# A one-core decoder step: scores with zero-padded queries, heads convolved in pairs, stores behind loads, filler matmuls, shared sample tiles

## The chip, the cores and the metric

The kernel runs on one core of one Trainium2 chip. The metric is the device time of one execution in microseconds (us); the executions shown agree within 0.3%. PE is TensorE, DVE VectorE, ACT ScalarE, POOL GpSimd; SP is the engine from whose queue all DMAs are issued here.

## The reference

One inference step of a hybrid decoder layer: a prompt of 512 tokens and eight samples of four tokens, 544 rows of width 1024 in all.

```python
shift, scale, gate = split(silu(c) @ w_cond + b_cond, 3)
h = x * (1 + scale) + shift
qa, ka, va, za, qkv_b, zb, a_b, b_b, g_a, g_b = h @ w_in          # 11280 columns
# branch A: dilated sliding-window softmax attention, 3 groups of 8 heads of 64,
#   (window, dilation) = (128, 1), (512, 4), (2048, 16); the groups merged by softmax share; * silu(za)
# branch B: causal convolution of width 4 + silu on q, k, v; gated delta rule over 8 heads of 128,
#   exact, in chunks; RMS norm per head; * silu(zb)
merged = sigmoid(g_a) * (yA @ w_branch_a) + sigmoid(g_b) * (yB @ w_branch_b)
y = layer_norm(ALPHA * x + gate * (merged @ w_out))
```

It also returns the key and value rows of the windows (those of the samples are the caches moved on by four rows, the bulk of the writes), the last three rows ahead of the convolution, and the delta states.

## The kernel before

The kernel doesn't issue instructions as its Python runs. `Recorder` (line 246) records every operation with its tiles; `schedule` (line 426) then plans all five engines with a cost model of its own, and `emit` (line 644) issues each engine's operations in the planned order. That is why every instruction of the profile has line 663. At each step the planner takes the engine that is free first, and on it the ready operation with the lowest rank, then the earliest recorded. Ranks: 0 the recurrence of branch B, 1 its blocks, 2 gates and preparation, 3 prompt attention, 4 early sample attention, 9 the stream of projections (on engines other than PE these go first, rank -1), 30 the copies of the caches. On PE an operation of another array mode than the present one may be held back for up to `HOLD`, 1 us of the plan. The threads of the recording (`Threads`, line 673) are interleaved by a clock that counts planned PE time.

**The stream.** `jobs` (line 1978) holds one entry for each 128 columns of the projection. A job loads 512 KB of weights (`wt`, three buffers), splits them into a rounded part and a rest (`hi` on ACT, `lo` on DVE, two buffers each), and multiplies them with `hhi` and `hlo`, the split activations, in two halves of 272 columns, 24 matmuls each. Each half goes to one of the two banks of `pp` and is copied out by `evac`. The order of jobs before: head 0 of branch B, then for each of four head pairs j nine attention jobs (query, key, value of three groups), with heads 1, 2 after the first nine, 3, 4 after the second, 5, 6 after the third, and head 7 between the sixth and the seventh of the last nine. The jobs for `za`, `zb` and the gates follow.

**The front.** Eight modulation tiles `wm` of 1 MB are loaded and multiplied (`cond_product`), the activations made from the result, and the first three jobs run ahead, tile by tile.

**Branch B.** `conv_job` (line 1085) copies a projection into `ext` (two buffers), convolves it on DVE into `acc` (two buffers), and writes head h's `KQ` (two buffers) or `uv` (one buffer). `delta_blocks` (line 1133) prepares the 128-row chunks; `delta_rule` (line 1244) runs the recurrence over four chunks, head after head. The job that makes the first part of head h starts, in the recording, when head h-2 is through.

**Branch A.** `attention_job` (line 1380) copies query, key and value out: for groups 1 and 2 in a permuted order. The 128 rows of a tile are two heads of 64. `scores` (line 1433) takes for each head the rows `hp` of query and key, a contraction of 64 rows, so PE is in a mode of half its rows (64\*128 in the profile; other matmuls of 128 rows are 128\*128). Sixteen steps of six such matmuls, each in two passes, make 192 records. After probabilities, transposes and value products the groups are merged with weights that go through DRAM (`dw`, `wv`).

**Samples.** `sample_attention` (line 1601) runs twice; the early one keeps its tiles in nine slabs of `opool` and, for `Qz` and `PTa`, in a pool `s0`.

Of the kernel before, what the change touches and what calls it, by code (L numbers as in the profile page):

```python
# [21 lines left out]
SEQ = 512  # L22
# [223 lines left out]
class Recorder:  # L246
# [5 lines left out]
    AGAIN = {"pe": 0.0, "ve": 0.11, "se": 0.14, "ge": 0.11, "sp": 0.0}  # L252
    HOLD = 1.0
    ENTER = {(128, 128): 0.197, (64, 128): 0.197, (64, 64): 0.142, (32, 32): 0.073, (128, 64): 0.1, (128, 32): 0.0,
             (64, 32): 0.1, (32, 128): 0.2, (32, 64): 0.1}
# [3 lines left out]
    def __init__(self):  # L259
        self.ops, self.events, self.rank, self.now, self.idle = [], [], 0, 0.0, 0.0  # L260
        self.group = None
        self.hold = self.HOLD
        self.scratch = {}


# [79 lines left out]
    def cost(self, op, args):  # L345
# [35 lines left out]
        elif e == "se":  # L381
            c = (0.155 if in_psum else 0.21) + 0.83e-3 * n
            a = (0.07 if "accum_out" in op.kw else 0.0) + (0.08 if pointer else 0.0)
            op.cost, op.late = c - 0.1 + a, 0.1
            f = args[2]
# [5 lines left out]
        else:  # L391
# [20 lines left out]
            if not dram[0]:  # L412
                per, op.extra = run / 23.3e3, 1.75
# [9 lines left out]
            op.cost, op.late, op.table = 0.53 if dram[0] and dram[1] else 0.42, 0.0, None  # L423


    def schedule(self):
# [30 lines left out]
        avail = {e: [] for e in self.ENGINES}  # L457
        free = {e: 0.0 for e in self.ENGINES}
        port, queue, table = {"ve": 0.0, "ge": 0.0}, {True: 0.0, False: 0.0}, None
# [64 lines left out]
        while done < len(ops):  # L524
            best = None
            for e in self.ENGINES:
# [111 lines left out]
        events()  # L638
        self.span = max(op.done for op in ops)

    def margin(self, p, op):
# [74 lines left out]
def body(ctx, tc, io):  # L716
# [47 lines left out]
    ones = consts.tile([128, 128], F32, name="ones")  # L764
    ve.memset(ones, 1.0)
    small = consts.tile([128, 4], F32, name="small")
    bnw, hbnw, eps4, eps1 = (small[:, i:i + 1] for i in range(4))
# [44 lines left out]
    with ExitStack() as fctx:  # L812
# [14 lines left out]
        for k in range(KT):  # L827
            sp.dma_start(wm[k], io["w_mod"][k])
            if k == 0:
                sp.dma_start(cst, io["const"])  # L830
            if k % 2 == 0:
                sp.dma_start(xT[:, k:k + 2], io["xT"][:, k:k + 2])
            if k in FIRST:
                i = FIRST.index(k)
                raws[i] = wraw.tile([128, D], F32, name="wt", tag="wraw")
                sp.dma_start(raws[i], io["w_in"][TILE_AT["b", 0, (1, 0, 2)[i]]])
        sp.dma_start(wab, io["w_ab"])
        sp.dma_start(tables["g"], io["const_g"])
# [294 lines left out]
    def delta_blocks(h):  # L1133
# [14 lines left out]
        rcf = rc.rearrange("p a c -> p (a c)")  # L1148
        kr = dl.tile([128, 4, 128], F32, name="kr")
        for s in range(2):  # L1150
# [3 lines left out]
            sq = dl.tile([128, 4, 128], F32, name="sq", bufs=1)  # L1154
            for c in range(4):
                se.activation(sq[:, c], cols128(pt)[:, c], AF.Square, accum_out=rc[:, s, c:c + 1])
            if s == 0:
                ve.tensor_copy(kr, cols128(pt))
            yield 2.2 + 2 * s
# [13 lines left out]
        yield 1.0  # L1173
        QKd = dl.tile([128, 4, 128], F32, name="QKd")
        ve.tensor_mul(QKd, NTs, cols128(rb[:, 1]))
# [204 lines left out]
    def attention_job(j, g, s):  # L1380

        def begin():
            pairs[j][s, g] = spare()[:, :SEQ] if s == 2 else ap.tile([128, 512], F32, name="qk"[s], bufs=3)

        def evac(n, ps):
            t, scale = pairs[j][s, g], 1.0 if s else -0.125
            if g == 0:
                lo, hi = ((0, 272), (272, 512))[n]
                se.activation(t[:, lo:hi], ps[:, 0:hi - lo], AF.Copy, scale=scale)
            else:  # L1390
                v = t.rearrange("p (r a n) -> p n a r", r=4, a=4)
                m = (17, 15)[n]
                se.activation(v[:, 17 * n:17 * n + m], ps[:, 0:16 * m].rearrange("p (n a r) -> p n a r", a=4, r=4),
                              AF.Copy, scale=scale)
            if n:
# [6 lines left out]
    def prompt_attention():  # L1402

        for j in range(4):
            qt, kt, vrow = {}, {}, {}
            for g in range(3):
                yield ready[j, g]
                qt[g], kt[g], vt = (pairs[j][s, g] for s in range(3))
                vrow[g] = ap.tile([128, 4, 128], F32, name="vrow", bufs=3)
# [23 lines left out]
            def scores(i):  # L1433
# [4 lines left out]
                for g in range(3):  # L1438
                    for hh in range(2):
                        hp = slice(64 * hh, 64 * hh + 64)  # L1440
                        if g == 0:
                            pe.matmul(pS[hh][:, k0:256], qt[0][hp, tk], kt[0][hp, 128 * (i - 1) + k0:128 * (i + 1)],
                                              start=True, stop=True)
# [157 lines left out]
    def sample_attention(T, t, stream, W, pace_of, by, over):  # L1601


        cols = slice(256 * T, 256 * T + 256)
        Qz = t["Qz"].rearrange("p (g j i h) -> p g j i h", g=3, j=2, h=4)
        ge.memset(Qz, 0.0)
        for jl in range(2):
            for hh in range(2):
                hp = slice(64 * hh, 64 * hh + 64)
                ge.tensor_copy(Qz[hp, :, jl, :, 2 * jl + hh], qs[hp, 2 * T + jl])  # L1610

# [42 lines left out]
        for jl in range(2):  # L1654
            for x in range(1024 // W):
                kt = kts[jl, x]
                for bl in range(0, nb, 2):
                    b = nb * x + bl
                    pe.matmul(pS[16 * b:16 * b + 32, 0:256], Qz[:, 0, jl, 4 * b:4 * b + 8].rearrange("p i h -> p (i h)"),
                              kt[:, 128 * bl:128 * bl + 256], start=(jl == 0), stop=(jl == 1), tile_position=(0, 16 * b))  # L1660
        for g in range(3):
            for jl in range(2):
                for bp in range(4):
                    pe.matmul(pS[32 * bp:32 * bp + 32, 256 + 32 * g:288 + 32 * g],
                              Qz[:, g, jl, 8 * bp:8 * bp + 8].rearrange("p i h -> p (i h)"), ks[:, 2 * T + jl, g, :],
                              start=(jl == 0), stop=(jl == 1), tile_position=(0, 32 * bp))
# [68 lines left out]
    def early_tiles():  # L1735

        slab = [op.tile([128, NT], F32, name="slab", tag="o") for _ in range(9)]
        t = {}
        for i, names in ((4, ("Sa", "qr", "sst")), (5, ("Sb", "od", "o2")), (6, ("sba", "PTn")), (7, ("sbb", "om")), (8, ("knv",))):
# [237 lines left out]

    for s in (1, 0, 2):
        jobs.append(conv_job(0, s))
    h = 1  # L1980
    for j in range(4):
        nine = [attention_job(j, g, s) for g in range(3) for s in range(3)]
        if j == 3:
            jobs += nine[:6] + [conv_job(7, s) for s in (1, 0, 2)] + nine[6:]
        else:
# [17 lines left out]
    ap = pool(actx, "ap", 1)  # L2003
    s0ctx = ExitStack()
    s0 = pool(s0ctx, "s0", 1)
    threads.set(began, 0.0)
# [18 lines left out]
    threads.run(lambda: not threads.parts)  # L2025
    s0ctx.close()
    actx.close()
# [12 lines left out]
    def samples():  # L2040
        yield from sample_decays(op.tile([128, NT], F32, name="nd", tag="o"))
        yield from sample_delta()
        s1 = pool(sctx1, "s1", 1)
        yield from sample_attention(1, {n: qr1 if n == "qr" else s1.tile([128, w], F32, name=n) for n, w in SHAPES.items()},
                                    lambda: s2.tile([128, D], F32, name="kv", tag="cache"), 1024, 2.0, (ve,), late_over)
# [248 lines left out]
```

## Time and profile before

| | us |
|---|---|
| median of three runs | 958.55 (956.23 to 959.11) |
| the profiled execution | 957.46 |
| its span, first to last instruction | 955.5 |
| PE busy | 915.9 |
| DVE busy | 738.5 |
| ACT busy | 417.6 |
| POOL busy | 61.9 |

Granted clock of PE over the span: 0.984. Bytes read from HBM 220.49 MB, written 103.70 MB. In a row of the profile stand the engine, the operation, the tiles written and read, the shapes and a count; fp32 matmuls take two passes and so appear twice. Durations of matmuls overlap, since they are pipelined: what one costs is seen from start to start.

### The profile page before, as it was taken

Reading aid. Unit: us, or ns where it says so; the run is one execution under the profiler, and the core shown is the slowest. Engines: PE = TensorE matmul, PEld = TensorE weight load, DVE = VectorE, ACT = ScalarE, POOL = GpSimd, SP = SyncE. Lnnn points to the kernel's source line nnn. Section 1 sums busy time; section 2 is a strip of 40 time slices with the busy share of each in tenths; the row PEclk is TensorE's granted clock in tenths of the full one; section 3 lists DMA queues with packets and bytes.
Section 4 is the critical chain, followed back from the end, with each engine's and each line's share of the span. In section 5 each row is a group of like instructions: output and inputs, shape, how many; then the busy total and the mean of one; then the engine's idle time right before and its main releaser. Section 6 shows DMA issues by size and latency. Waiting matters only on the chain.

```text
span 955.5 us, 20831 instructions
## 1 busy us (share of the span) xinstructions
PE 915.9 (96%) x8134; PEld 844.6 (88%) x8134; DVE 738.5 (77%) x1635; ACT 417.6 (44%) x981; POOL 61.9 (6%) x176
## 2 busy tenths in 40 slices
PE   6999999999989999999999799998999999999895
PEld 4889989999879999889998699897999999988685
DVE  4474556876879999799989857655889798978658
ACT  3363457553547443556544445441442222234421
POOL 0110001100000200011200000001010000000000
PEclk9999999999989999999999799999999999999998
DMA  9676745676778777978787646459869899987513
GB/s 364 256 234 191 246 154 185 215 250 186 247 257 279 236 262 226 320 266 301 222 297 241 218 161 197 164 151 345 287 223 373 317 400 396 354 312 284 186 39 113
DMA packets 104565, 237.87 MB, mean 249 GB/s; under 512 B 29890, under 2 KB 61260, under 8 KB 100756
## 3 DMA queue, kind: packets, MB, share of 16 engines
q1 hardware_dynamic: 104468, 236.55, 72.6%
q8 instruction: 64, 1.05, 0.4%
q14 instruction: 33, 0.27, 0.1%
HBM read 220.49 MB, written 103.70 MB: 339 GB/s over the span
## 4 chain that ended last, share of the span: by engine, by line
PE 71%; DVE 17%; DMA 5%; ACT 3%; issue 2%; SPq 1%; DVEq 0%; ACTq 0%
PE pp L663 53%; PE pg L663 9%; PE pd L663 7%; PE pb L663 3%; DVE slab L663 2%; DVE r L663 2%; DVE lo L663 2%; DVE acc L663 1%; SPq L663 1%; DMA slab<-in_vs 1%; DVE tmp L663 1%; DVE Tb L663 1%; DMA wv<-dw 1%; DMA wm<-in_w_mod 1%; DVE XF L663 1%
## 5 line engine op out<-in xcount | busy, mean ns | idle before, releaser
L663 PE MATMUL pp<-hhi,hi 128*128 128x272 f32 x1360 | 402.6, 296 | 6.2 <-DVE zt L663 3.3
L663 PE MATMUL pp<-hhi,lo 128*128 128x272 f32 x1360 | 403.0, 296 | 0.0
L663 PE MATMUL pp<-hlo,hi 128*128 128x272 f32 x1360 | 401.3, 295 | 0.0
L663 PEld LDWEIGHTS pp<-hhi,hi 128*128 128x128 f32 x1360 | 259.0, 190 | 9.3 <-DVE zt L663 3.7
L663 PEld LDWEIGHTS pp<-hlo,hi 128*128 128x128 f32 x1360 | 259.4, 191 | 2.1 <-issue 1.1
L663 PEld LDWEIGHTS pp<-hhi,lo 128*128 128x128 f32 x1360 | 258.7, 190 | 2.6 <-issue 1.4
L663 ACT ACTIVATE hi<-wt 128x1024 fp32r<-128x1024 f32 (+1 forms) x102 | 104.7, 1027 | 173.3 <-PE pp L663 134.4
L663 DVE TENSOR_TENSOR lo<-wt,hi 128x1024 fp32r<-128x1024 f32 (+1 forms) x102 | 120.0, 1176 | 40.5 <-ACT hi L663 35.4
L663 DVE SCALAR_TENSOR_TENSOR acc<-ext,cw,acc 128x568 f32<-128x568 f32 x72 | 57.5, 800 | 4.1 <-ACT acc L663 3.7
L663 ACT ACT_TABLE_LOAD x36 | 46.2, 1283 | 7.2 <-DVE acc L663 4.8
L663 DVE TENSOR_TENSOR slab<-slab 128x512 f32<-128x512 f32 (+1 forms) x66 | 42.7, 665 | 5.2 <-DMA slab<-in_vs 3.0
L663 DVE TENSOR_REDUCE slab<-slab 128x8 f32<-128x512 f32 (+2 forms) x66 | 42.6, 658 | 0.3
L663 ACT ACTIVATE P<-P,st 128x256 f32<-128x256 f32 (+1 forms) x64 | 31.2, 488 | 22.2 <-DVE st L663 21.7
L663 ACT ACTIVATE zt<-pp 128x272 f32<-128x272 f32 x48 | 18.6, 389 | 46.8 <-PE pp L663 34.6
L663 PE MATMUL pp<-ybh,hi 128*128 128x272 f32 x128 | 37.0, 289 | 0.0
L663 PE MATMUL pp<-ybl,hi 128*128 128x272 f32 x128 | 36.8, 288 | 0.0
L663 PE MATMUL pp<-ybh,lo 128*128 128x272 f32 x128 | 36.8, 287 | 0.0
L663 PE MATMUL pg<-k,q 64*128 64x128 f32 (+1 forms) x192 | 30.1, 328 | 0.1
L663 ACT ACTIVATE ext<-pp 128x272 f32<-128x272 f32 (+2 forms) x66 | 18.3, 316 | 23.4 <-PE pp L663 19.9
L663 POOL COPY cx<-ext 128x3 f32<-128x3 f32 (+1 forms) x48 | 22.2, 492 | 89.0 <-ACT ext L663 88.9
L663 DVE TENSOR_TENSOR Tb<-Tb,tmp 32x15 f32<-32x15 f32 (+7 forms) x120 | 23.4, 195 | 4.1
L663 PE MATMUL pg<-cst,P 128*128 128x128 f32 x120 | 25.1, 294 | 1.5 <-DVE st L663 1.5
(405 smaller groups left out, 1658.8 us busy)
## 6 DMA issues: line engine op xcount, KB each, us to landing
out_kv_s<-in_cache SPq DMA_DIRECT2D x144, 512.0 KB
wt<-in_w_in SPq DMA_DIRECT2D x88, 512.0 KB
out_kv_s<-in_cache SPq DMA_DIRECT2D x24, 496.0 KB
wm<-in_w_mod SPq DMA_DIRECT2D x8, 1024.0 KB
slab<-in_ks SPq DMA_DIRECT2D x32, 256.0 KB
slab<-in_vs SPq DMA_DIRECT2D x32, 256.0 KB
kv<-in_ks SPq DMA_DIRECT2D x16, 512.0 KB
kv<-in_vs SPq DMA_DIRECT2D x16, 512.0 KB
```

Of the source, the lines that this page charges most:

```text
L663: getattr(real[x.engine], x.name)(*map(arg, x.args), **{k: arg(v) for k, v in x.kw.items()})
```

## The change

Five edits, and three figures of the planner's cost model.

- Queries are copied out twice, each head's 64 rows into a tile of its own, `padded[g][hh]`, whose other 64 rows stay zero. Scores contract over all 128 rows.
- The convolution jobs stand in pairs: heads 0, 1, then nine attention jobs, heads 2, 3, nine, 4, 5, nine, 6, 7, nine.
- A DMA that writes an output gets rank 20, behind all loads.
- `warm`: where the plan leaves PE idle, with no PE operation known to be ready within 0.25 us, and PE planned busy for at most 3.0 of the last 3.413 us, it adds a matmul of a tile of ones, 128 by 128, into a spare bank that nothing reads.
- Tiles of the early sample attention share rows of the slabs; pool `s0` goes, and in `delta_blocks` `sq` becomes `QKd`.
- The planner counts a strided ACT output as dearer, front loads as faster, and small DMA issues as longer, and lets PE start at 1.2 us.

```diff
+        if name == "dma_start" and not isinstance(args[0], View) and op.rank < 20:
+            op.rank = 20
...
+            x = self.warm(wait["pe"], avail["pe"], free["pe"], best, busy, state) if held.get("pe") is None else None
+            if x is not None:
+                push(avail["pe"], prio(x) + (x,))
+                best = (free["pe"], "pe")
...
+    def warm(self, wait, avail, at, best, busy, state):
+        if avail or best is None or best[0] < at or best[1] == "pe" and best[0] <= at:
+            return None
+        if wait and wait[0][0] < at + self.GAP:
+            return None
+        heat = sum(b - max(a, at - 3.413) for a, b in busy[-400:] if b > at - 3.413)
+        if heat > self.HEAT:
+            return None
+        for pool, tag in self.spare:
...
+            op = self.add("pe", "matmul", (v[:, 0:128], self.ones, self.ones), dict(start=True, stop=True))
...
+            return op
+        return None
...
     def attention_job(j, g, s):
...
+            for t, hp in [(pairs[j][s, g], slice(0, 128))] if s else [(padded[g][hh], slice(64 * hh, 64 * hh + 64))
+                                                                     for hh in range(2)]:
...
-                            pe.matmul(pS[hh][:, 128 + 128 * g:256 + 128 * g], qt[g][hp, tk], kt[g][hp, tk],
+                            pe.matmul(pS[hh][:, 128 + 128 * g:256 + 128 * g], qt[g][hh][:, tk], kt[g][:, tk],
                                       start=True, stop=True)
...
-        for n in ("Qz", "PTa"):
-            t[n] = s0.tile([128, SHAPES[n]], F32, name=n)
+        t["sba"], t["PTa"] = t["Sa"], t["Sa"][:, 0:256]
+        t["om"], t["PTn"] = t["sbb"], t["sbb"][:, 0:128]
+        t["Qz"] = [slab[7][:, 256:512], slab[6][:, 0:512]]
...
-    for s in (1, 0, 2):
-        jobs.append(conv_job(0, s))
-    h = 1
-    for j in range(4):
-        nine = [attention_job(j, g, s) for g in range(3) for s in range(3)]
-        if j == 3:
-            jobs += nine[:6] + [conv_job(7, s) for s in (1, 0, 2)] + nine[6:]
-        else:
-            jobs += nine + [conv_job(h + i, s) for i in range(2) for s in (1, 0, 2)]
-            h += 2
+    at = [0, 0, 9, 9, 18, 18, 27, 27]
+    attn = [attention_job(j, g, s) for j in range(4) for g in range(3) for s in range(3)]
+    for i in range(37):
+        jobs += [conv_job(h, s) for h in range(8) if at[h] == i for s in (1, 0, 2)] + attn[i:i + 1]
...
+    padded = [[ap.tile([128, 512], F32, name=f"q{g}{hh}") for hh in range(2)] for g in range(3)]
+    for g in range(3):
+        for hh in range(2):
+            ge.memset(padded[g][hh][64 - 64 * hh:128 - 64 * hh], 0.0)
```

More of the change, by code (lines that the diff above doesn't have):

```diff
@@ L263, in __init__ @@
         self.scratch = {}
+        self.front = True
     def engines(self):
@@ L383, in cost @@
             a = (0.07 if "accum_out" in op.kw else 0.0) + (0.08 if pointer else 0.0)
+            ix = op.outs[0].ix
+            if n > 16 and ix.ndim > 1 and abs(int(ix.flat[1]) - int(ix.flat[0])) > 4:
+                a += 1.0e-3 * n
             op.cost, op.late = c - 0.1 + a, 0.1
@@ L412, in cost @@
             if not dram[0]:
-                per, op.extra = run / 23.3e3, 1.75
+                per, op.extra = run / (26e3 if self.front else 23.3e3), 1.75
                 if isinstance(args[1], View):
@@ L423, in cost @@
             op.cost, op.late, op.table = 0.53 if dram[0] and dram[1] else 0.42, 0.0, None
+            sbuf = [v for v in op.outs + op.ins if v.base.pool.side != "dram"]
+            if sbuf and sbuf[0].shape[0] <= 32 and min(runs) < 2048:
+                op.cost = 0.68
     def schedule(self):
@@ L457, in schedule @@
         avail = {e: [] for e in self.ENGINES}
-        free = {e: 0.0 for e in self.ENGINES}
+        free = {e: 1.2 if e == "pe" else 0.0 for e in self.ENGINES}
         port, queue, table = {"ve": 0.0, "ge": 0.0}, {True: 0.0, False: 0.0}, None
@@ L639, in schedule @@
         self.span = max(op.done for op in ops)
+    def warm(self, wait, avail, at, best, busy, state):
[7 more added lines that the diff above has]
+        for pool, tag in self.spare:
+            key = (id(pool), tag)
+            s = state.get(key)
+            if not pool.open or s is None or not s["slots"] or s["wait"] or min(s["slots"]) + self.WAKE["pe"] > at:
+                continue
+            v = pool.tile([128, 512], F32, name="warm", tag=tag)
+            v.base.bufs = pool.bufs
+            self.rank, self.group = 40, None
+            op = self.add("pe", "matmul", (v[:, 0:128], self.ones, self.ones), dict(start=True, stop=True))
+            self.rank = 0
+            t = v.base
+            t.turn, t.left, t.line, t.given = {}, 1, None, True
+            t.free = max(s["slots"].pop(s["slots"].index(min(s["slots"]))), pool.since)
+            for x in (t, self.ones.base):
+                x.pool.left += 1
+            self.ones.base.left += 1
+            op.left, op.banks, op.ready, op.group = 0, [t], at, None
+            self.warmed = getattr(self, "warmed", 0) + 1
+            return op
+        return None
     def margin(self, p, op):
@@ L765, in body @@
     ve.memset(ones, 1.0)
+    rec.ones, rec.spare = ones, [(psb, "b"), (psg, "g"), (psd, "d")]
     small = consts.tile([128, 4], F32, name="small")
@@ L1149, in delta_blocks @@
         kr = dl.tile([128, 4, 128], F32, name="kr")
+        QKd = dl.tile([128, 4, 128], F32, name="QKd")
         for s in range(2):
@@ L1404, in prompt_attention @@
         for j in range(4):
-            qt, kt, vrow = {}, {}, {}
+            qt, kt, vrow = padded, {}, {}
             for g in range(3):
                 yield ready[j, g]
-                qt[g], kt[g], vt = (pairs[j][s, g] for s in range(3))
+                kt[g], vt = (pairs[j][s, g] for s in (1, 2))
                 vrow[g] = ap.tile([128, 4, 128], F32, name="vrow", bufs=3)
@@ L1604, in sample_attention @@
         cols = slice(256 * T, 256 * T + 256)
[L1605 to L1610, printed above, removed]
+        Qz = []
+        for q in t["Qz"]:
+            ge.memset(q, 0.0)
+            g0, q = len(Qz), q.rearrange("p (g j i h) -> p g j i h", j=2, i=32, h=4)
+            n = q.shape[1]
+            Qz += [q[:, g] for g in range(n)]
+            for jl in range(2):
+                for hh in range(2):
+                    hp = slice(64 * hh, 64 * hh + 64)
+                    ge.tensor_copy(q[hp, :, jl, :, 2 * jl + hh], qs[hp, 2 * T + jl, g0:g0 + n])
         knv = t["knv"][0:96].rearrange("p (u c) -> p u c", u=2)
@@ L1738, in early_tiles @@
         t = {}
-        for i, names in ((4, ("Sa", "qr", "sst")), (5, ("Sb", "od", "o2")), (6, ("sba", "PTn")), (7, ("sbb", "om")), (8, ("knv",))):
+        for i, names in ((4, ("Sa", "qr", "sst")), (5, ("Sb", "od", "o2")), (7, ("sbb",)), (8, ("knv",))):
             at = 0
@@ L2003, in body @@
     ap = pool(actx, "ap", 1)
-    s0ctx = ExitStack()
-    s0 = pool(s0ctx, "s0", 1)
+    padded = [[ap.tile([128, 512], F32, name=f"q{g}{hh}") for hh in range(2)] for g in range(3)]
+    for g in range(3):
+        for hh in range(2):
+            ge.memset(padded[g][hh][64 - 64 * hh:128 - 64 * hh], 0.0)
     threads.set(began, 0.0)
@@ L2043, in samples @@
         s1 = pool(sctx1, "s1", 1)
-        yield from sample_attention(1, {n: qr1 if n == "qr" else s1.tile([128, w], F32, name=n) for n, w in SHAPES.items()},
+        yield from sample_attention(1, {n: qr1 if n == "qr" else [s1.tile([128, w], F32, name=n)] if n == "Qz"
+                                        else s1.tile([128, w], F32, name=n) for n, w in SHAPES.items()},
                                     lambda: s2.tile([128, D], F32, name="kv", tag="cache"), 1024, 2.0, (ve,), late_over)
```

37 lines of the change are left out of this document (18 added, 19 removed).

## The prediction

> **What bounds the kernel now.** I read the page first, then busy time by windows, TensorE's waits, and the timeline around each loss.
>
> ```profile
> span 955.5 us, 20831 instructions
> PE 915.9 (96%) x8134; PEld 844.6 (88%) x8134; DVE 738.5 (77%) x1635; ACT 417.6 (44%) x981; POOL 61.9 (6%) x176
> PE 71%; DVE 17%; DMA 5%; ACT 3%; issue 2%; SPq 1%; DVEq 0%; ACTq 0%
> ```
>
> TensorE (PE) is busy for 915.9 of 955.5 us and holds 71% of the chain that ended last. So a microsecond off PE's own work is a microsecond off the end, and work for the other engines is free until PE waits for it. What can be won beside PE's work is the 39.6 us in which PE is idle and the time in which its clock is low. The windows place both.
>
> ```profile
> 0.00:6.90 6.90, 0.00 (x0) 0.01 (x1) 1.15 (x7) 1.70 (x2) 0.20 (x4) 1.00 0.67 228
> 6.90:24.40 17.50, 15.84 (x88) 11.01 (x89) 8.57 (x20) 6.25 (x11) 0.00 (x0) 1.00 1.02 420
> 24.40:40.10 15.70, 15.70 (x162) 12.04 (x161) 6.16 (x21) 4.25 (x9) 0.00 (x0) 1.00 0.90 351
> 40.10:47.20 7.10, 7.10 (x57) 7.10 (x58) 3.60 (x9) 3.15 (x9) 2.34 (x11) 1.00 0.16 36
> ...
> 266.70:270.10 3.40, 1.66 (x15) 1.15 (x13) 3.30 (x7) 0.00 (x0) 0.19 (x1) 1.00 1.28 447
> 270.10:276.90 6.80, 5.60 (x26) 5.63 (x27) 4.92 (x15) 4.86 (x19) 0.24 (x2) 0.50 0.86 298
> ...
> 536.40:546.60 10.20, 7.39 (x31) 6.57 (x31) 8.01 (x12) 3.70 (x16) 2.02 (x7) 0.50 0.74 229
> ...
> 614.90:618.30 3.40, 3.40 (x20) 3.03 (x19) 1.76 (x8) 2.07 (x8) 0.00 (x0) 0.50 0.00 0
> ...
> 652.40:655.80 3.40, 3.40 (x18) 3.40 (x17) 1.31 (x5) 0.00 (x0) 0.93 (x3) 0.50 1.10 334
> ```
>
> After the first busy column come PEld, DVE, ACT and POOL, then granted clock, DMA share, GB/s. The clock is halved in four stretches, with 5.60, 7.39, 3.40 and 3.40 us of PE work in them; half of that, 9.9 us, is what the low clock costs there. The first 24.4 us are slow too, although the column says 1.00 (it has no record that early): pairs of the same matmul follow each other 0.46 us apart at 22.72 and 0.25 us apart at 24.46.
>
> ```profile
> 22.72 0.66 PE L663 MATMUL pg<-hhi,wlo 128*128 128x272 f32 x2
> 23.18 0.66 PE L663 MATMUL pg<-hlo,whi 128*128 128x272 f32 x2
> ...
> 24.46 0.42 PE L663 MATMUL pp<-hlo,whi 128*128 128x272 f32 x2
> 24.71 0.41 PE L663 MATMUL pg<-hhi,whi 128*128 128x272 f32 x2
> ```
>
> The waits of PE are few; the columns are total, times and longest, and after the start the longest is 3.3 us:
>
> ```profile
> PE pp L663 <- DVE zt L663: 4.1, 3, 3.3
> PE pp L663 <- ACT ext L663: 2.3, 1, 2.3
> ...
> PE pd L663 <- DVE z L663: 1.9, 2, 1.7
> PE pd L663 <- DVE U L663: 1.6, 1, 1.6
> ...
> PE pb L663 <- ACT kq L663: 1.2, 1, 1.2
> ```
>
> **The change part by part.** The profiled execution took 957.46 us, 1.96 around its span, and stands 1.1 below the median of 958.55. The sum is made against 957.46. About 0.3% (2.9 us) is what a measurement can tell from no change.
>
> *Matmuls of ones, start.* PE's first work waits 6.9 us for a load and runs at half clock until 24.4.
>
> ```profile
> L663 PE MATMUL pd<-wm,cs x128: 378/403/636, 6.9 to 39.7; 128*32 128x256 f32 x128
> ```
>
> Fillers from 1.2 us on would bring the full clock before or soon after that first work. Up to half of the 15.84 us can go, 7.9. But the loads bound it: they move 228 x 6.9 = 1.6 MB and 420 x 17.5 = 7.4 MB by 24.4 us, and then 351 GB/s; by their shapes in the code the eight modulation tiles, x and three weight tiles are 12.2 MB, so the last lands near 33.5 us (an estimate from these rates). PE works on it until 39.7, late by its own backlog, and has this stage behind it at 47.2, 7.5 us later. With no backlog the last load's product ends near 34 us, a little over 1 us after it lands, and the stage near 41. So the gain lies between 0 (the fillers do not raise the clock, or stand in the way) and 6; I take 5, as the first third of the work may still run slow.
>
> *Matmuls of ones, later.* The planner puts them only where its own plan has an idle PE, not where the chip has one. What they could save is the 9.9 us of low clock, less what the next parts remove by themselves; what they cost is two passes of a 128-column matmul each wherever PE is not idle after all. The price is read here:
>
> ```profile
> 290.35 0.39 PE L663 MATMUL pd<-vn,QKd 128*128 128x128 f32 x2
> 290.57 0.39 PE L663 MATMUL pd<-S,KQ 128*128 128x128 f32 x2
> ```
>
> The second pair of passes starts 0.22 us after the first, so a filler is 0.22 us and forty of them in the wrong place are 9 us. I take a net -1, with ends -6 and +9. The window of 266.7 shows that short gaps are enough to lose the clock: PE was busy for 1.66 of 3.4 us, in waits of which the longest was the 1.6 on U, and the next window runs at half. The Trainium skill, "TensorE: Matmul & The Clock Gate", section "Why this matters for your kernels", asks only that gaps between bursts stay under about 3 us. By it just the start and the 3.3 us wait at 649 could cool the array, and this term would be at most the 1.7 us after 652; the trace disagrees with it at 266.7, so the row stands.
>
> *Zero-padded queries.* A score matmul used half the rows of the array (64\*128); now it uses all, with zeros in the other head's half, and the mode is that of its neighbours.
>
> ```profile
> L663 PE MATMUL pg<-k,q 64*128 64x128 f32 x144 | 20.9, 294 | 0.1
> L663 PE MATMUL pg<-k,q 64*128 64x256 f32 x48 | 11.9, 429 | 0.0
> ...
> 63.41 1.03 PE L663 MATMUL pb<-KQ 128*128 128x256 f32 x4
> 64.09 0.47 PE L663 MATMUL pp<-hhi,hi 128*128 128x272 f32 x1
> 64.41 0.29 PE L663 MATMUL pp<-hlo,hi 128*128 128x272 f32 x1
> ...
> 291.90 1.14 PE L663 MATMUL pg<-k,q 64*128 64x256 f32 x6
> 292.97 0.33 PE L663 MATMUL pg<-cst,P 128*128 128x128 f32 x1
> ...
> 405.55 1.15 PE L663 MATMUL pg<-k,q 64*128 64x256 f32 x12
> 406.63 0.40 PE L663 MATMUL pp<-hhi,hi 128*128 128x272 f32 x1
> 406.86 0.29 PE L663 MATMUL pp<-hlo,hi 128*128 128x272 f32 x1
> ```
>
> Now: 20.9 + 11.9 = 32.8 us. After: in full mode a 256-column pass takes (64.41 - 63.41 - 0.125) / 4 = 0.22 us, a 128-column one 0.11, so 48 x 0.22 + 144 x 0.11 = 26.4. That is 6.4 less, and a further 0.1 us after each run of scores, since the first matmul of the next mode starts its successor 0.23 us later where 0.125 is usual (406.63). Against it, a run that stands next to value products or small triangular blocks keeps one change of mode. I take 5, ends 2 and 9. A rule speaks against this edit: "TensorEngine Tiling (Array Packing)", section "When to Use Tiling", of the Trainium skill, gives twice the speed to contractions of 64 when two row tiles run at once. By it all scores would now take half of 26.4, and padding would cost 13. The trace bears it out only where both heads of a step stand together: twelve passes in 1.08 us at 405.55, but six passes, half as many, in 1.07 us at 291.90; the sum of 32.8 holds both kinds, so the term goes by it, and the rule as a case of its own has no chance here.
>
> ScalarE now copies each half of the queries by itself, with the same columns:
>
> ```profile
> L663 ACT ACTIVATE q<-pp 128x272 f32<-128x272 f32 x12 | 6.9, 576 | 19.3 <-PE pp L663 19.3
> ```
>
> That is up to 24 x 0.58 = 14 us more on an engine that is 44% busy. A half job has 24 matmuls at 0.125, 3.0 us, and there are two banks; two copies take 1.2. They are hidden, and cost up to 14 if nothing covers them; I take +1 for weight splits that queue behind them. POOL's six memsets and four extra small copies wait for nobody (6% busy).
>
> *Heads in pairs.* Job order is now h0 h1, attention 0, h2 h3, attention 1, and so on. Heads 1, 3, 5 move nine jobs earlier, 7 six earlier, attention 0 to 2 three later. The largest loss of the trace lies at head 7, which today follows heads 5 and 6 after six jobs:
>
> ```profile
> 538.25 0.63 PE L663 MATMUL pd<-S,KQ 128*128 128x128 f32 x2
> ...
> 540.13 1.22 DVE L663 SCALAR_TENSOR_TENSOR KQ<-ext,acc 128x512 f32<-128x512 f32 x2
> 540.79 0.75 ACT L663 ACTIVATE ext<-pp 128x272 f32<-128x272 f32 x3 [1.10 <-DVE KQ L663]
> ...
> 541.24 0.59 PE L663 MATMUL pp<-hhi,hi 128*128 128x272 f32 x1 [2.35 <-ACT ext L663]
> ```
>
> Read upward from the last: PE waits for a bank, the bank for `ext`, `ext` for the writes to KQ, and those for head 5's recurrence to let KQ go (two buffers; its last reader is at 538.25). With the waits for kq and z just before, the idle time is 2.35 + 1.2 + 1.7 = 5.3 us, and half of 7.39 is lost to the clock: 9.0. In pairs every head follows its buffer's owner after fifteen jobs, as heads 3 to 6 do today, so I let this go whole. What is late next: head 1's three jobs follow head 0's at once and want `ext`, of which there are two, while VectorE still works on head 0; I price that at +2 (two waits like the 1.2 above), ends 0 and 5. The next loss, 3.3 + 1.7 around 652, I leave: the last attention job keeps its place and its weights' round trip through DRAM. Sum of this part -7, ends 0 and -14 (the losses at 266 to 277 and 652 gone as well, 5 of them).
>
> *Stores behind loads.* Stores of outputs now yield on SP to loads that are ready. What waits behind them is the buffer they read: above all the key rows' copy (`spare`, two buffers), which the next value job wants.
>
> ```profile
> 252.03 1.82 SPq L663 DMA_DIRECT2D out_kv_p<-spare  x4
> ```
>
> An issue is 0.46 us; four loads let past are 1.8 us on a buffer that is wanted 6 us later. 0, ends -1 and +2. *Sample tiles sharing rows:* the tiles are used one after the other in any case; 0.
>
> *A newly planned order.* All engines' orders are written anew; small waits (the list above from 1.9 down) come back elsewhere. I put +1 there.
>
> Sum: -5 - 1 - 5 + 1 - 7 + 0 + 1 = -16, 957.46 - 16 = 941.5.
>
> **The rivals.** *Losses move, they do not go:* pairs bring as much waiting as head 7 had (0 for that part), and the rest stays: 957.5 - 9 = 948.5. For it: VectorE is at 77% over all and cannot be relieved, only shifted. Against: the pairs of today lose less than head 7. *More goes than I count:* the losses at 266 to 277 (half of 5.60, and the 1.7 idle before it) and around 652 (5.0) too, the start to its bound: 941.5 - 4.5 - 5 - 1 = 931. *Slower:* the KQ wait repeats at each pair. A second head's recurrence ends later than its KQ buffer is wanted two jobs on; from there each pair pays 9.0, three pairs 27 where one such loss stood. 957.5 + 27 - 9.0 - 10 (scores and start) = 965.5. For it: recurrences are a serial chain by head, and head 1's starts only when head 0's is through. Against: fifteen jobs of about 6 us and the attention between them. *Fillers in the way:* the plan's idle time is not the chip's, 9 us or more come back and the start gives nothing: 941.5 + 5 + 10 = 956.5, no change.
>
> **How the numbers follow.** Forecast 941.5: 0.58 (its own range 933 to 948). Losses move, 948.5: 0.17. More goes, 931: 0.12. No change, 956.5: 0.05. Slower, 965.5: 0.08. Faster by over 0.3% is 0.58 + 0.17 + 0.12 = 0.87, same 0.05, slower 0.08. The range runs from 927 to 956; it leaves out the slower case and a little at each end.
>
> **What would show it.** Right: the matmuls with 272 columns at 0.125 us steps before 15 us, and the stage of the modulation done near 42; no 64\*128 matmul, and scores near 26 us; no wait of `ext` on KQ at the last head; one or two half-clock stretches, not four. Wrong: fillers standing between ready matmuls while the PE row is full; new PE waits on `ext` or KQ near heads 1, 3 or 5; a longer stretch between the last attention job and the first zb job.

## The result, and the profile after

The changed kernel takes 928.33 us (median of 4 runs, 925.99 to 930.22), the kernel before 957.39 beside it on the same chip (4 runs, 951.05 to 959.11, so they spread wider than the 0.3% that the prediction allowed for noise): a ratio of 0.9707, 95% interval 0.9654 to 0.976. The forecast was 941.5 with a range of 927 to 956, so the sign was right and the range held, but the gain came out at 29 us where 16 were forecast, outside the forecast's own 933 to 948 and close to the rival "more goes than I count" (931). The profiled execution took 929.9, with a span of 928.1 against 955.5.

The page first: span, busy time of the engines, and the chain that ended last.

```profile
span 928.1 us, 20971 instructions
PE 907.1 (98%) x8168; PEld 847.6 (91%) x8168; DVE 737.6 (79%) x1635; ACT 435.2 (47%) x1007; POOL 78.7 (8%) x187
PE 79%; DVE 11%; DMA 5%; ACT 2%; issue 2%; SPq 0%; DVEq 0%; ACTq 0%
```

PE's busy time fell by 8.8 us only, its idle time from 39.6 to 21.0. The waits of PE after (total, times, longest) show that nearly nothing is left between the start and 610 us:

```profile
PE pd L707 <- DMA wm<-in_w_mod: 2.9, 2, 2.1
PE pp L707 <- DVE lo L707: 2.1, 1, 2.1
PE pp L707 <- DVE spare L707: 2.0, 1, 2.0
PE warm L707 <- DVE ones L707: 1.0, 1, 1.0
PE pb L707 <- DVE QKd L707: 0.6, 1, 0.6
PE pp L707 <- DVE zt L707: 0.5, 1, 0.5
```

No `ext` and no `kq` is among them, and z and U are gone. The windows in which the kernel before lost its clock, or stood, now read as follows (columns as in the prediction: busy PE, PEld, DVE, ACT and POOL, clock, DMA share, GB/s); the two at the end are the only half-clock stretches left before the kernel's tail:

```profile
266.70:276.90 10.20, 10.20 (x114) 10.02 (x113) 6.26 (x14) 6.42 (x17) 0.54 (x1) 1.00 0.88 267
536.40:546.60 10.20, 9.88 (x92) 8.41 (x92) 8.25 (x33) 3.46 (x8) 0.20 (x1) 1.00 1.01 319
652.40:655.80 3.40, 3.40 (x30) 3.40 (x29) 3.40 (x6) 2.32 (x3) 0.00 (x0) 1.00 1.02 354
614.60:618.00 3.40, 3.40 (x17) 3.40 (x16) 0.00 (x0) 0.56 (x1) 0.00 (x0) 0.50 0.99 405
874.00:877.40 3.40, 3.40 (x9) 2.63 (x8) 3.40 (x5) 1.06 (x1) 0.00 (x0) 0.50 0.43 143
```

To place the gain I cut each profile at two points that every kernel here has: the first copy of a wide product of head 0 (`ext`, which ends the modulation stage) and the start of the last matmul. One window between the two, for the kernel before and then for the changed one:

```profile
46.20:945.20 899.00, 878.05 (x7840) 815.45 (x7838) 711.77 (x1563) 402.90 (x954) 60.34 (x166) 0.99 0.73 247
```

```profile
44.70:917.30 872.60, 866.46 (x7842) 814.81 (x7841) 710.80 (x1563) 420.40 (x980) 76.46 (x174) 1.00 0.77 255
```

The same matmuls stand in both (7840 records). Length less busy is PE's idle time: 20.9 before, 6.1 after. Half of the PE work inside half-clock stretches is what the clock cost: 9.9 before, (3.40 + 3.40) / 2 = 3.4 after. What is left I call net work: 878.05 - 9.9 = 868.2 before, 866.46 - 3.4 = 863.1 after. So the 27.4 us of span are 1.5 from an earlier end of the modulation stage, 14.8 of idle time, 6.5 of low clock and 5.1 of net work, less 0.5 at the tail.

Two of the parts look other than they were meant to. The matmuls of ones stand at the start alone, 17 of them in two passes each, and later the planner placed none:

```profile
L707 PE MATMUL warm<-ones x34: 272/421/583, 1.0 to 21.1; 128*128 128x128 f32 x34
```

And the padded scores are busier than the half-row ones, not less: 24.3 + 14.6 = 38.9 us by form where 20.9 + 11.9 = 32.8 stood.

```profile
L707 PE MATMUL pg<-k,q 128*128 128x128 f32 x144 | 24.3, 283 | 0.0
L707 PE MATMUL pg<-k,q 128*128 128x256 f32 x48 | 14.6, 386 | 0.0
```

### The profile page after: what moved, and what is told of

It is laid out like the page before. It is cut to its first block, busy times and chain, and to the rows that moved or that the text cites. A ratio compares the mean times of both kernels' runs of the same rounds, so it can differ in the third digit from the quotient of the medians.

```text
span 928.1 us, 20971 instructions
## 1 busy us (share of the span) xinstructions
PE 907.1 (98%) x8168; PEld 847.6 (91%) x8168; DVE 737.6 (79%) x1635; ACT 435.2 (47%) x1007; POOL 78.7 (8%) x187
## 4 chain that ended last, share of the span: by engine, by line
PE 79%; DVE 11%; DMA 5%; ACT 2%; issue 2%; SPq 0%; DVEq 0%; ACTq 0%
PE pp L707 55%; PE pg L707 11%; PE pd L707 8%; PE pb L707 3%; DVE r L707 2%; DVE lo L707 2%; DVE slab L707 1%; DMA wt<-in_w_in 1%; DMA wm<-in_w_mod 1%; DVE tmp L707 1%; DVE Tb L707 1%; DMA wv<-dw 1%; DMA rb<-dr 1%; ACT L707 1%; DMA dO<-vr 1%
## 5 line engine op out<-in xcount | busy, mean ns | idle before, releaser
L707 POOL COPY cx<-ext 128x3 f32<-128x3 f32 (+1 forms) x48 | 32.3, 703 | 70.8 <-ACT ext L707 70.7
L707 PE MATMUL pg<-k,q 128*128 128x128 f32 (+1 forms) x192 | 35.7, 309 | 0.0
L707 PEld LDWEIGHTS pg<-k,q 128*128 128x128 f32 x192 | 27.8, 191 | 3.0 <-issue 1.4
L707 ACT ACTIVATE q<-pp 64x272 f32<-64x272 f32 (+1 forms) x48 | 26.3, 549 | 8.5 <-PE pp L707 8.0
L707 DVE CUSTOM_DVE_ANT_0 P<-pg,bias 128x256 f32<-128x256 f32 (+1 forms) x64 | 24.0, 401 | 3.7 <-PE pg L707 3.3
```

Source lines behind the costliest of these rows:

```text
L707: getattr(real[x.engine], x.name)(*map(arg, x.args), **{k: arg(v) for k, v in x.kw.items()})
```

## The experiments

The theory: the new order of the jobs takes the waits and the low clock away, by the KQ buffers, and the other parts are worth a few us each. The rivals: the padded scores (or the planner's new figures, which the prediction had not priced) carry the gain; or any newly made plan moves the time by several us, so that no part can be named. Each ratio is to the kernel before, run beside it on the same chip (its medians lay between 955.7 and 957.4).

| kernel | us | ratio, 95% interval | idle | low clock | net work |
|---|---|---|---|---|---|
| before | 957.39 | 1 | 20.9 | 9.9 | 868.2 |
| changed | 928.33 | 0.9707 (0.9654 to 0.976) | 6.1 | 3.4 | 863.1 |
| order_only | 941.67 | 0.9828 (0.98 to 0.9855) | 6.6 | 1.7 | 874.4 |
| all_but_order | 947.45 | 0.9891 (0.9867 to 0.9916) | 17.9 | 5.5 | 869.6 |
| shared_kq3 | 942.06 | 0.9862 (0.9836 to 0.9887) | 11.6 | 3.4 | 870.0 |
| padded_shared | 961.06 | 1.0052 (1.0026 to 1.0078) | 22.3 | 11.9 | 867.5 |
| all_but_padded | 939.04 | 0.9832 (0.9801 to 0.9863) | 9.9 | 1.7 | 874.4 |
| halves_frozen | 936.66 | 0.9813 (0.9785 to 0.9842) | 5.3 | 0 | 873.9 |
| all_but_figures | 936.60 | 0.9805 (0.9774 to 0.9836) | 9.7 | 3.4 | 866.5 |
| front_figures | 925.92 | 0.9699 (0.9674 to 0.9724) | 4.2 | 0 | 864.5 |
| all_but_fillers | 930.33 | 0.9742 (0.9707 to 0.9776) | 5.4 | 0 | 867.6 |
| replan_before | 950.05 | 0.9908 (0.988 to 0.9936) | 12.4 | 8.0 | 871.7 |
| replan_after | 925.84 | 0.9688 (0.9659 to 0.9717) | 7.6 | 0 | 862.2 |
| replan_nofill | 933.64 | 0.9769 (0.9747 to 0.9791) | 6.9 | 1.7 | 867.0 |

The last three columns (us) are from the profiled execution, worked out as above between the same two points.

**How far a mere re-plan moves the time.** One planner constant is nudged; the work stays the same. First in the kernel before, then in the changed one:

```
-    WAKE = {"pe": 0.06, ...
+    WAKE = {"pe": 0.08, ...
```

> The kernel before with one planner constant nudged: the wake-up time that it reckons for TensorE is 0.08 us in place of 0.06 us. The work is the same, the order of instructions is planned anew. Theories 1 and 2: within 3 us of 957. Theory 3 (the plan moves freely): a difference of 5 us or more either way, idle time of TensorE at other places; it would set the size below which no part's own run can be read.

> The changed kernel with the wake-up time that the planner reckons for TensorE nudged from 0.06 to 0.08 us: same work, order planned anew. The same nudge moved the kernel before by -6 us. If the changed kernel's plan is an ordinary one: 928 us within 6 us either way. If it is a lucky one: 934 us or more, and then up to 6 us of the change's gain belongs to no part of it. If the nudged constant is itself truer to the chip (waits planned longer, as they are): faster here too, 922 to 926 us.

Measured: the kernel before gains 0.9% (about 9 us by the ratio, 6 by the medians) from nothing but another plan, and the changed one is at 0.9688 against 0.9707, inside the interval. The trace of the first says what it gained: the wait around 652 us is gone, while the last head's stretch stays.

```profile
528.80:539.00 10.20, 9.24 (x43) 5.47 (x44) 8.13 (x16) 4.59 (x12) 0.42 (x2) 0.50 0.76 239
542.40:545.80 3.40, 3.40 (x46) 3.11 (x45) 2.66 (x5) 1.26 (x4) 0.18 (x2) 0.50 0.62 183
```

So the rival of the free plan holds for up to some 9 us by these two nudges (others were not tried), and a difference below that tells of a part only if the plan is held fixed or the trace shows the place.

**The order alone, and all but the order.** The first is the kernel before with the new job list, the second the changed kernel with the old one.

```
-        nine = [attention_job(j, g, s) for g in range(3) for s in range(3)]
...
+    at = [0, 0, 9, 9, 18, 18, 27, 27]
...
+        jobs += [conv_job(h, s) for h in range(8) if at[h] == i for s in (1, 0, 2)] + attn[i:i + 1]
```

> The kernel before, with only the new order of the jobs: head convolutions in pairs ahead of attention chunks 0, 9, 18 and 27. Theory 1 (the order is the gain): TensorE's idle time between 47 and 653 us, 17.6 us before, falls to under 6 us, two or more of the four half-clock stretches of before go, the 9 us of waits around 532 to 541 us are gone, and the time falls by 12 to 20 us, to 937 to 945 us beside 957. Theory 2 (the scores and the planner's figures are the gain, the order only moves the waits): idle time in that stretch stays above 12 us, and the time falls by less than 6 us. Theory 3 (any newly made plan moves the time by several us either way): a result anywhere from -10 to +5 us with the idle time at places that neither theory names.

> The changed kernel with the old order of the jobs. Theory 1 (the order is the gain): 12 to 20 us slower than the changed kernel, 941 to 949 us, with the wait of the last head's convolution for its KQ buffer back near 515 to 540 us. Theory 2 (the scores and the figures are the gain): within 6 us of the changed kernel, under 935 us. Theory 3 (the plan moves freely): between the two, with the idle time elsewhere.

Measured: 1.7% faster alone, and 1.8 points (17 to 19 us) slower when left out. Both are twice what a re-plan moved, and the places agree. With the order alone:

```profile
266.70:276.90 10.20, 10.20 (x141) 9.68 (x140) 4.26 (x10) 7.56 (x20) 1.79 (x3) 1.00 0.99 314
530.00:550.00 20.00, 20.00 (x248) 18.88 (x248) 17.64 (x47) 7.39 (x14) 0.99 (x4) 1.00 0.70 200
884.80:888.20 3.40, 3.40 (x10) 2.62 (x9) 3.40 (x6) 1.06 (x1) 0.00 (x0) 0.50 0.31 96
```

Without it, in the changed kernel, the loss at the last head is back, and so is one before the zb jobs:

```profile
530.60:537.40 6.80, 5.77 (x53) 5.49 (x54) 4.53 (x9) 2.07 (x7) 0.61 (x4) 0.50 0.37 119
643.20:650.10 6.90, 5.30 (x23) 5.30 (x24) 1.51 (x5) 1.35 (x3) 1.89 (x4) 0.51 1.11 330
```

The theory holds: the order removes 14.3 us of idle time and 8.2 of low clock. The net work speaks against a plain sum, though: alone, the order adds 6.2 us of it.

**Is it the KQ buffer?** The kernel before with a third KQ buffer; the sample tiles are shared as in the change, to make room for it. Old order, old scores.

```
-        hd.KQ = dl.tile([128, 4, 2, 128], F32, name="KQ")
+        hd.KQ = dl.tile([128, 4, 2, 128], F32, name="KQ", bufs=3)
```

> The kernel before with the shared sample tiles (to make room) and a third KQ buffer; old order, old scores, old figures. Theory of the prediction (the last head's stall comes from the KQ buffer of head 5): no wait of ext on KQ, TensorE loses under 2 us between 505 and 550 us (6.4 before, 4.5 to 8.8 in the other three kernels with the old order), no half-clock stretch there, 946 to 951 us. Rival (VectorE, busy for 38.8 of 45 us there, is late by itself with three heads behind one another, and the KQ buffer is only the last thing it is late for): other waits on VectorE stand in its place, over 4 us lost there, a half-clock stretch stays, 952 to 960 us.

Measured: 0.9862, as good as the order alone within the intervals, and better than my theory asked. The stretch around the last head, first in the kernel before, then with three buffers:

```profile
505.00:550.00 45.00, 38.63 (x338) 34.27 (x339) 38.80 (x99) 21.41 (x56) 3.90 (x14) 0.89 0.67 219
```

```profile
505.00:550.00 45.00, 44.14 (x471) 40.66 (x471) 39.12 (x100) 22.80 (x63) 7.89 (x14) 1.00 0.72 233
266.70:276.90 10.20, 9.81 (x78) 8.13 (x76) 9.61 (x24) 6.20 (x17) 1.36 (x2) 1.00 1.00 341
```

VectorE is as busy as it was (38.80 and 39.12 of 45 us), and PE no longer stands: 133 more matmuls fit into the stretch. That is against the rival that VectorE is simply late there. Other kernels agree: in all four profiles with the old order and two KQ buffers (before, replan_before, padded_shared, all_but_order) PE waits for `ext` at the last head, 2.35 us in the first and 1.21 us in each of the others; in those with the new order or a third buffer it waits there for 0.35 us at most. In padded_shared, which shares the tiles as well, ScalarE's copy into `ext` waits 2.5 us for KQ, and the half-clock stretch stays:

```profile
522.10:549.40 27.30, 20.44 (x139) 13.99 (x139) 21.06 (x44) 10.24 (x24) 1.88 (x7) 0.50 0.72 234
```

The half-clock stretch at 266 to 277 is gone as well with the third buffer, but it isn't shown to hang on KQ. The kernel all_but_order, with two buffers and the old order, has no PE wait over 0.3 us between 47 and 327 us either; and in the kernel before PE waits there for results of VectorE (U, then st), which is busy for 3.30 of the 3.40 us from 266.7 on. A plan that orders VectorE's work otherwise may be all it takes. What the shared tiles alone do was not run; since a re-plan gave 0.9908, some of the 0.9862 may be the plan's.

**The padding.** Four kernels bear on it. Padding alone, with the tiles that make room for it, in the old order with the old figures; and the changed kernel with the scores of before:

> The kernel before with the zero-padded queries and the shared tiles that make room for them; old job order, old figures of the planner, no matmuls of ones, stores queued as before. By the prediction's terms (-5 us for the scores, +1 us for ScalarE's second copy) 953 us beside 957. Theory 1 (the order is the gain): -2 to -7 us, the waits around 532 to 541 us still there. Theory 2 (the scores are the gain): -10 us or more. The busy time of the score matmuls should read 35 to 36 us as in the changed kernel, 32.8 before, so that a gain shows only in mode changes and waits.

> The changed kernel with the scores of before (half the rows of the array, queries in one tile, one copy by ScalarE). The prediction's terms (-5 for scores, +1 for the copies) ask for 4 us more than the changed kernel, 932 us. The rival that the padding costs time, as it did alone (about +5 us beside the kernel before), asks for 4 to 6 us less, 922 to 925 us. A rival of planning alone: within 3 us either way, with the score matmuls' busy time back at 33 us and idle time moved.

Measured: alone it is 0.5% slower, where the prediction's terms asked for a gain; left out of the change it costs 1.3 points (10.7 us by the medians). The signs differ, and so do the net works: 868.2 to 867.5 in the old order, where padding brings next to nothing; 874.4 to 863.1 in the new one, where it brings 11. To take the plan out of it, the third kernel keeps every instruction of the changed one in its place on every engine, and only lets each score matmul read its own 64 rows:

```
-                            pe.matmul(pS[hh][:, ...], qt[g][hh][:, tk], kt[g][:, tk], ...
+                            pe.matmul(pS[hh][:, ...], qt[g][hh][hp, tk], kt[g][hp, tk], ...
```

(and the planner still reckons them as 128 rows).

> The changed kernel, every instruction of every engine in the same place of the same order, but each score matmul reads its own half of the rows (64 rows of the padded query tile and of the keys) in place of all 128 with zeros. The plan is held fixed, so nothing but the mode of the array differs. If the padding's gain is the change of mode itself: the score matmuls go from 28.1 us start to start back to 31 to 33, the matmuls around them lose a further 4 to 7 us, and the kernel is 6 to 12 us slower than the changed one, 934 to 940 us. If the gain of 10.7 us seen when padding was left out was the luck of another plan: within 3 us of 928.

Measured: 936.66 us, 0.9813 against 0.9707, with 10.8 us more net work. That is the mode of the array and nothing else; the time differs by less (8.3 us by the medians), since this profile has 3.4 us less of low clock and 0.8 less of idle time. The scores take 33.2 us from start to start in place of 28.1, and most of the remaining 5.7 us falls to the matmuls right ahead of them and behind them. Two places of the two traces show how it goes. A single product between projections, first padded, then in half rows:

```profile
551.98 0.29 PE L707 MATMUL pp<-hhi,lo 128*128 128x272 f32 x1
552.10 0.38 PE L707 MATMUL pg<-k,q 128*128 128x128 f32 x2
552.24 0.37 PE L707 MATMUL pp<-hhi,hi 128*128 128x272 f32 x1
552.45 0.27 PE L707 MATMUL pd<-z,XF 128*128 128x128 f32 x1
```

```profile
560.91 0.29 PE L707 MATMUL pp<-hhi,lo 128*128 128x272 f32 x1
561.13 0.49 PE L707 MATMUL pg<-k,q 64*128 64x128 f32 x2
561.54 0.40 PE L707 MATMUL pp<-hhi,hi 128*128 128x272 f32 x1
561.78 0.27 PE L707 MATMUL pd<-z,XF 128*128 128x128 f32 x1
```

From the projection ahead to the second matmul behind: 552.45 - 551.98 = 0.47 us padded, 0.87 in half rows. Here the padding saves 0.4 for one product. A run of twelve passes goes the other way, padded and in half rows:

```profile
431.20 2.02 PE L707 MATMUL pg<-k,q 128*128 128x256 f32 x12
433.15 0.44 PE L707 MATMUL pd<-Tc,NTs 32*32 32x32 f32 x16
```

```profile
439.33 1.59 PE L707 MATMUL pg<-k,q 64*128 64x256 f32 x12
440.86 0.44 PE L707 MATMUL pd<-Tc,NTs 32*32 32x32 f32 x16
```

It takes 1.95 us padded and 1.53 in half rows. These two are the ends. The two traces have the same 48 runs of scores, and from the matmul ahead to the second one behind, idle gaps left out, padding saves:

| products in the run | runs | saved in all, us | per run, us |
|---|---|---|---|
| 1 | 21 | 5.1 | 0.24 |
| 2 | 12 | 2.8 | 0.23 |
| 3 | 12 | 3.0 | 0.25 |
| 4, 5, 6 | 3 | -0.7 | -0.25, 0, -0.43 |

So up to three products the saving goes by the run and not by the product, which fits a cost of changing the mode at the run's two ends. Only in the longest runs do the half rows win that back, and there are three. What padding is worth thus depends on how finely the plan cuts the scores. In the kernel before the 192 passes stand in 37 runs, 12 of them a single product; with the new order alone in 53 runs, 30 of them single. (Counted in the order of the matmuls in the trace.) By the table padding should save about 5 us on the 37 runs, if they stood still (an estimate); padded_shared, planned anew with 47 runs, shows 0.7. The finer cut into 53 runs is where the 6.2 us of added net work of the order alone comes from, for the most part: from one matmul's start to the next's, summed over all score passes with idle gaps left out, the scores take 27.9 us before, 32.9 with the order alone and 28.1 in the changed kernel. Why the planner cuts them finer in the new order was not tried.

**The planner's figures.** The change also corrects costs in the planner: PE free from 1.2 us on, a faster rate for the first loads, dearer strided writes of ScalarE, dearer issues of small DMAs. The prediction did not price them. All four set back, then only the last two:

```
-        free = {e: 1.2 if e == "pe" else 0.0 for e in self.ENGINES}
+        free = {e: 0.0 for e in self.ENGINES}
...
-                per, op.extra = run / (26e3 if self.front else 23.3e3), 1.75
+                per, op.extra = run / 23.3e3, 1.75
```

> The changed kernel with the planner's old figures (TensorE free from 0, ScalarE's strided writes and the small DMA issues at their old costs, the old rate for the first loads). The prediction gave no term to them beyond +1 for a new plan: 928 us, within 3 us. The rival that the better figures carry what the padding and order do not (the changed kernel in old order is 13.6 us faster than padding alone, and 2 to 3 of that are fillers): 6 to 12 us more, 934 to 940 us, the idle time of TensorE in small waits on ScalarE's copies.

> The changed kernel with the planner's old costs for ScalarE's strided writes and for small DMA issues, but the new ones for the start (TensorE free from 1.2 us, 26 instead of 23.3 GB/s for each DMA engine in the first loads). All four old ones together cost 8.3 us. If the figures of the start bring the front's gain: the first wide copy stays at 44 to 45 us (46.4 with all old ones), and the kernel is at 928 to 934 us. If the other two carry the 8.3: 934 to 938 us. A re-plan alone moves 3 to 6 us, so only an end of this range would tell.

Measured: 0.9805 with the old four, 0.9699 with the two of the start alone (925.92 us, below the range expected). The last two are worth nothing that can be measured. With all four old ones the first `ext` comes at 46.4 us, with those of the start at 44.6 and 44.7 (46.2 before), which is 1.8 of the 10.7 us between the two. But that isn't the figures alone: with PE free from 0 the planner placed only nine matmuls of ones, the first at 8.7 us in place of 1.0, so the run changes the ones too. Most of the rest is idle time (9.7 against 4.2 and 6.1) that is spread over the whole kernel in the plan without them, and is not told apart from a re-plan.

**The matmuls of ones.** Left out of the changed kernel, and left out under the nudged constant:

```
-        if avail or best is None or best[0] < at or ...
+        if True or avail or best is None or best[0] < at or ...
```

> The changed kernel with no matmul of ones. The prediction's term (-5 at the start, -1 later) asks for 6 us more than the changed kernel, 934 us. The reading of the trace after (17 fillers, all before 21.1 us, full clock from 17.2 in place of 24.4 us, first wide copy 44.7 in place of 46.2 us) asks for 2 to 3 us more, 930 to 931 us, with the late clock stretches unchanged. A rival: the fillers are worth nothing, since loads bound the start: 928 us.

> The changed kernel with the wake-up time nudged to 0.08 us and no matmul of ones. With fillers that plan took 925.8 us. If the fillers are worth nothing (without them the first wide copy came no later, 43.5 against 44.7 us): 923 to 928 us. If they are worth the 2 us by which leaving them out missed the changed kernel: 927 to 929 us. By the prediction's -6: 932 us.

Measured: 0.9742 against 0.9707 with them, intervals overlapping; and 0.9769 against 0.9688, 7.8 us by the medians, where the second is slower than any of the cases expected. The traces do not give the ones that much. The first `ext` comes at 43.5 us without them in the first pair (44.7 with) and at 45.6 in the second (44.3 with): once a loss of 1.2, once a gain of 1.3. In the first pair the full clock came as early as with them; in the second, pairs of 272-column matmuls still follow each other 0.45 us apart at 22.27,

```profile
22.27 0.66 PE L707 MATMUL pg<-hhi,whi 128*128 128x272 f32 x2
22.72 0.66 PE L707 MATMUL pg<-hhi,wlo 128*128 128x272 f32 x2
```

and in the changed kernel 0.47 apart at 16.94 and 0.24 apart from 20.06:

```profile
16.94 0.63 PE L707 MATMUL pp<-hhi,wlo 128*128 128x272 f32 x2
17.41 0.41 PE L707 MATMUL pp<-hlo,whi 128*128 128x272 f32 x2
...
20.06 0.41 PE L707 MATMUL pp<-hhi,wlo 128*128 128x272 f32 x2
20.30 0.41 PE L707 MATMUL pp<-hlo,whi 128*128 128x272 f32 x2
```

Without ones, the plan doesn't settle when the full clock comes. The kernel with three KQ buffers has none, and up to the end of the modulation stage every engine has the same instructions in the same order as the kernel before. There pairs followed each other 0.46 us apart as late as 22.72; here they are 0.25 apart from 19.33 on, and the first `ext` comes at 44.5 us in place of 46.2:

```profile
19.33 0.41 PE L699 MATMUL pp<-hlo,whi 128*128 128x272 f32 x2
19.58 0.41 PE L699 MATMUL pg<-hhi,whi 128*128 128x272 f32 x2
```

So the 1.5 us by which the changed kernel's stage ended earlier are no more than the same instructions show between two executions. What the ones may bring is an even start: in the six profiles that have them from 1.0 us on the first `ext` comes at 44.1 to 44.7 us, in the seven without any at 43.5 to 46.2, a mean of about 1 us later (an estimate from these profiles). One profiled execution of each is too few to be sure.

The remaining 6 us of the second pair lie in the middle, where no matmul of ones stands in either, as net work (867.0 against 862.2) and low clock. They go with the plan, not with the ones.

The stores behind loads and the shared tiles were not run by themselves.

## Why the prediction came out as it did

*Start, -5:* over-sized. The stage ended 1.5 us earlier, not 5 to 6. The step that failed is that fillers from 1.2 us on bring the full clock "before or soon after that first work": PE was at half clock until past 16.94 us with them. The products of two of the eight modulation tiles ran at half clock, where three did before. Whether the ones moved the stage's end at all stays open, since the same instructions without ones ended it at 46.2 and at 44.5 us.

*Matmuls of ones later, -1:* none was placed, so neither the gain nor the price of 9 us could arise. With the old order the planner does place some after the start, the last at 637.9 us in its profile; with the new order its plan has no gap that wants one.

*Zero-padded queries, -5:* net work fell by 5.1 between the two kernels, and the number is right by accident. It was worked out from busy times (32.8 down to 26.4); those of the scores rose to 38.9, and still the kernel gained: records overlap (the two passes at 552.10 last 0.38 us, the next matmul starts 0.14 after them), so a group's busy time is no price. The step that failed is to set a price from start to start (26.4) against a busy time: from start to start the scores took 27.9 us before and 28.1 after. The 0.1 us behind each run, which the prediction added as a further small term, is what pays, and it was sized too small: about 0.24 us for each run of up to three products. Between the old order's plans padding is worth 0.7 us of net work; with the changed kernel's plan held fixed it is worth 10.8, while the order itself adds 6.2. The rule that the prediction took from "TensorEngine Tiling (Array Packing)" of the Trainium skill is a gain of up to 2x for contractions of 64 rows or fewer, in the section "Theoretical Speedup". The run of twelve passes agrees in direction (1.53 us in half rows, 1.95 padded). It does not decide here, since 45 of the changed kernel's 48 runs hold three products or fewer.

*ScalarE's second copies, +1:* no cost is seen. ScalarE is busy 17.6 us longer over all, and neither `q` nor `hi` stands among the waits of PE.

*Heads in pairs, -7:* the mechanism was right, the size short by half. The last head's wait for its KQ buffer is gone with the order, and gone with a third buffer in the old order. The step that failed is "the next loss ... I leave", together with the +2 for head 1: the losses at 266 to 277 and at 652 went too, and the only wait on `ext` at the start is 0.6 us with the order alone (1.1 before). Order alone took 14.3 us of idle time and 8.2 of low clock, less 6.2 of added net work, 16.4 of span. Neither of the two further losses is shown to hang on the order or on KQ: the nudged kernel before is without the one at 652 in the old order, and all_but_order without the one at 266. This is the rival "more goes than I count", 931, which had a chance of 0.12, though not by its start. "Losses move", "fillers in the way" and "slower" have no support in the trace: neither KQ nor `ext` stands among PE's waits of the changed kernel.

*Stores, tiles, new order: 0, 0, +1.* The first two were not tested alone. The third was the weakest term: the two re-plans without any other change gave about -9 and -2 us by the ratios, as much as any part but the pairs and the padding; two are too few to tell a size or a sign ahead.

## What to carry to other kernels

When the head of a chain stands for a buffer, count in jobs how long its last owner keeps it; another order, or one buffer more, takes away the wait and the half-clock stretch behind it. When another loss goes at the same time, look for it in a kernel that still has the old buffer before you give it the same cause. Price a change of array mode by the run of matmuls and not by the matmul or by busy time, from the start of the matmul ahead to the second one behind: here it paid 0.24 us for each run of up to three products, and cost only in the longest. Where a planner writes the order, nudge a constant that changes no work before reading any part's own run, and hold the plan fixed where a part is to be priced.

## What was not expected of the hardware

The same wait may or may not cost the clock. In the changed kernel a wait of 2.07 us near the end is followed by a stretch at half clock, in which matmuls of 512 columns follow each other 0.42 us apart:

```profile
872.76 0.47 PE L707 MATMUL pp<-wo0h,mhi 128*128 128x512 f32 x1 [2.07 <-DVE lo L707]
...
873.76 0.43 PE L707 MATMUL pp<-wo0l,mhi 128*128 128x512 f32 x1
873.99 0.63 PE L707 MATMUL pp<-wo0h,mlo 128*128 128x512 f32 x1
874.41 0.63 PE L707 MATMUL pp<-wo0h,mhi 128*128 128x512 f32 x1
```

In the kernel with the frozen plan the same instructions wait the same 2.07 us, and the steps behind stay at 0.24:

```profile
880.70 0.47 PE L707 MATMUL pp<-wo0h,mhi 128*128 128x512 f32 x1 [2.07 <-DVE lo L707]
...
881.93 0.40 PE L707 MATMUL pp<-wo0h,mlo 128*128 128x512 f32 x1
882.17 0.40 PE L707 MATMUL pp<-wo0h,mhi 128*128 128x512 f32 x1
```

The changed kernel's own four executions split in the same way: 929.9 and 930.22 us at a granted clock of 0.993 and 0.992, 925.99 and 926.76 at 0.996. Ahead of the kernel's tail the half-clock stretches of these profiles last 3.4 us or a multiple (6.8, 10.2, 27.3), so where a wait falls among such periods may decide; that was not tried.
